# Low parts of split weights made by an accumulating DMA instead of VectorE's subtraction

## Chip, core and metric

The kernel runs on one core of one Trainium2 chip. The metric is the time of one execution on the device, in microseconds (us). A core has TensorE (PE in the profile, with its weight loads as PEld), VectorE (DVE), ScalarE (ACT), GpSimd (POOL) and SyncE (SP), which here issues the loads.

## What is computed

One layer of a diffusion backbone: a half-step SwiGLU feed-forward block, a token mixer (latent attention beside a gated chunk MLP), and a second half-step SwiGLU block. The change touches only weights of the two feed-forward blocks:

```python
def swiglu(h, w1, w3, w2):
    return (jax.nn.silu(h @ w1) * (h @ w3)) @ w2

def ffn_sublayer(h_in, shift, scale, gate, norm_w, w1, w3, w2):
    h = modulate(rms_norm(h_in, norm_w), shift, scale)
    return h_in + 0.5 * gate * swiglu(h, w1, w3, w2)
```

The model width is 1024 and the hidden width 2816, that is 22 blocks of 128. The first block works on 768 tokens (512 latent, 256 context), the second on the 512 latent ones. Everything is float32.

## The kernel before

**Split operands.** TensorE is fed in the type fp32r, which keeps fewer bits than float32. To keep the precision, every operand is held as a pair: a high part (the value rounded to fp32r) and a low part (the value minus its high part). A product is three matmuls (`mm3`): high by high, high weight by low activation, low weight by high activation. The third is the first that needs the weight's low part.

**Pairs.** `Stream.operand` makes the pair of one weight piece of 128x512: ScalarE copies the piece into the high tile (`oph`), and VectorE subtracts the high tile from the piece into the low tile (`opl`). There are five buffers of each (`OPS`), used in rotation. The piece comes from a `raw` buffer (three of them, 128x1024, so two pieces each) that SP fills from `wst` in memory, or from a `block` buffer (two of them, 128x2048) in the stages below.

**Order.** `Flow` is a queue of pieces to be made. At each slot of TensorE's work, `fill` makes as many new pairs as the slot before used up, so up to five pairs are alive, and the slot takes its pairs from the front. In the feed-forward stages every engine's instructions keep the order in which the program is written.

**Stages that the change touches.**
- *Plain up projections.* Hidden blocks 2 and 3 of the first feed-forward block (`plain_wants`): two weights of two pieces each, so 2 x 2 x 2 = 8 pairs. Each pair serves 24 matmuls. Before them come two hidden blocks that run while the inputs arrive; their results are taken over by ScalarE and VectorE (`evac_first`) at the start of this stage.
- *Down projections.* After some of the hidden blocks, a group of them is multiplied with its part of `w2` (`down_wants`, `down_flow`). The first feed-forward block has groups of 5, 5 and 6 hidden blocks in this form, the second 4, 4, 4, 4 and 2. A group of n takes 2n pairs, so 32 and 36 pairs.

**Stages around them.** The other hidden blocks use a Strassen-Winograd form (`Winograd`): from a `block` of four pieces GpSimd makes sums and differences (four additions for each hidden block: `s`, then three in place in `block`), all seven results are split with `Stream.operand`, and seven products are run. The wants of the down groups stand in the same `Flow` queue, behind the last two pieces of a hidden block. GpSimd issues no transfer in the kernel before.

Of the kernel before, what the change touches and what calls it, by code (L numbers as in the profile page):

```python
# [12 lines left out]
AF = mybir.ActivationFunctionType  # L13
ALU = mybir.AluOpType
# [103 lines left out]
class Stream:  # L118
# [19 lines left out]
    def split(self, dst, src, eng=None):  # L138
        self.pin(self.nc.scalar.copy(dst[0], src))
        self.pin((eng or self.nc.vector).tensor_sub(dst[1], src, dst[0].bitcast(F32)))  # L140
        return dst

    def pair(self):
        return [self.op_pool.tile([P, 512], F32R, tag=f"op{p}", bufs=self.op_bufs, name=f"op{p}_{self.nc.next_id()}") for p in "hl"]
# [29 lines left out]
def layer_kernel(ctx: ExitStack, tc: tile.TileContext, xT, wfirst, wst, wada, wuq, wkpe, cols, wrope, vnw, rope, out):  # L174
# [7 lines left out]
    st = Stream(nc, raws, opp, OPS, wst)  # L182
# [81 lines left out]
    u0, rw0 = st.raw_pool.tile([P, 2048], F32, tag="block", bufs=BLOCKS, name="block_first"), st.raw()  # L264
# [48 lines left out]
    def ada_row(r, d, kts=range(NK)):  # L313
        n = 2 * P if d in ROWS2 else P
        o = pa[0:2, :n]
        for kt in kts:
            pin(nc.tensor.matmul(o, sc[:, kt, :], r[:, kt * n : kt * n + n], start=kt == 0, stop=kt == NK - 1))
        return o
# [210 lines left out]
    for k in range(NK):  # L529
# [13 lines left out]
        if later:  # L543
            o = ada_row(units[k + 2][0], k + 2)
# [82 lines left out]
    def down_wants(flow, n, u0):  # L627
        raw = []

        def want(p):  # L630
            if p % 2 == 0:
                raw[:] = [st.half(wst, u0 + p // 2)]
            return st.operand(raw[0][:, p % 2 * 512 : p % 2 * 512 + 512])

        for p in range(2 * n):
            flow.todo.append(lambda p=p: want(p))
# [27 lines left out]
    U_UP1, U_DN1, U_IN = 0, 44, 66  # L664
# [233 lines left out]
    flow = Flow(OPS)  # L898
# [3 lines left out]
    def plain_wants(f):  # L902
        for w in range(2):
            raw = []

            def first(w=w, raw=raw):
                raw[:] = [st.half(wst, U_UP1 + 2 * f + w)]
                return st.operand(raw[0][:, :512])

            flow.todo.append(first)  # L910
            flow.todo.append(lambda raw=raw: st.operand(raw[0][:, 512:]))

    for f in range(NFIRST, NPLAIN1):
        plain_wants(f)
# [166 lines left out]
    def in_want(i, w):  # L1081
        if w == 0:
            inw[i].append(st.half(wst, U_IN + i))
        src = inw[i][0][:, w * 512 : w * 512 + 512]
        inw[i].append(homes[2] if i == 2 and w else st.pair())
        hi, lo = inw[i][-1]
        nc.scalar.copy(hi, src)
        return lambda: nc.vector.tensor_sub(lo, src, hi.bitcast(F32))

    TILES = (0, 1, 2, 1, 2, 1, 1, 0)  # L1090
    for dt in range(NK):
        w = in_want(dt - 5, 0) if dt > 4 else None
# [212 lines left out]
    def v_norm(t, pt):  # L1305
        gv = ut[:, t, :]
        nc.scalar.activation(gv, pt, AF.Gelu_apprx_tanh)
        sq = p1.tile([P, 512], F32, tag="t3", name=f"sqg{t}")
        nc.scalar.activation(sq, gv, AF.Square)
        g4 = gv.rearrange("p (a b) -> p a b", a=4)  # L1310
        nc.gpsimd.tensor_mul(g4, g4, vw)
        m8 = p1.tile([P, 8], F32, tag="m8", name=f"m8g{t}")
        nc.vector.tensor_reduce(m8, sq.rearrange("p (h d) -> p h d", d=64), axis=AX.X, op=ALU.add)
        nc.vector.tensor_scalar(m8, m8, 1.0 / 64, EPS, ALU.mult, ALU.add)
        nc.gpsimd.tensor_tensor(m8, m8, nhalf, ALU.pow)
        vn = gv.rearrange("p (h d) -> p h d", d=64)
        nc.vector.tensor_mul(vn, vn, bc(m8.unsqueeze(2), [P, 8, 64]))
        split((vnh[:, t, :], vnl[:, t, :]), gv)
# [72 lines left out]
    def gate_t(j):  # L1391
        pt = mm()
        for t in range(4):
            nc.tensor.transpose(pt[:, t * P : t * P + P], ut[:, t, j * P : j * P + P], ident)
        split((mixh[:, j, :], mixl[:, j, :]), pt)
# [253 lines left out]
    def diffs(i):  # L1649
        hA1, hA2, hB1, hB2 = hfA[:, i, :], hfA[:, i + 4, :], hfB[:, i, :], hfB[:, i + 4, :]  # L1650
        nc.vector.tensor_sub(hA1, hB1, hA1)
        nc.vector.tensor_sub(hB1, hB2, hB1)
        nc.vector.tensor_sub(hB2, hB2, hA1)
        nc.vector.tensor_sub(hA2, hA2, hB2)
        split([d[:, i, :] for d in T1], hA1)
        split_shift([d[:, i, :] for d in T2], hB2, mod_s[2][0][:, i + 4 : i + 5])
# [37 lines left out]
    flow = Flow(OPS)  # L1694
# [142 lines left out]
```

## Time and profile before

| | |
|---|---|
| median of 3 runs | 1162.75 us (1162.31 to 1163.12) |
| the profiled execution's own time: its span, first to last instruction | 1160.9 us |
| the median stands above the span by | 1.85 us |
| instructions in the span | 18702 |
| transfers by SP and others, mean rate | 125.89 MB, 108 GB/s |

The page gives the busy time of each engine; TensorE's matmuls overlap, and their ends are modelled, so its busy share says little on whether it runs at its full rate. The number of matmuls that start in a window says more. In a timeline row stand the start, the duration, the engine, the line of the program, the operation and the tiles (out<-in), and in brackets the idle time of the engine before it and what ended it. Lines of the program that go through one helper are all shown as L60.

### The profile page before, as it was taken

What the parts mean: (1) busy time and instruction counts of PE and PEld (TensorE: products, weight loads), DVE (VectorE), ACT (ScalarE), POOL (GpSimd) and SP (SyncE); (2) the same over time, 40 slices, a digit from 0 to 9 for tenths busy, and PEclk for the clock granted to TensorE, in tenths of its full rate; (3) what the DMA queues carried; (4) which work ended last, traced back from release to release, by engine and by line L of the source; (5) the groups of instructions that cost most, each with busy time, mean ns of one, the idle gap of its engine ahead of it and who ended that gap; (6) DMA issues with size and microseconds to landing.
All of it is one profiled execution on the core that took longest, in us unless ns stands there. A gap on an engine that the chain in (4) does not pass through costs nothing. (4 is left out here: it accounts for less than half of the span.)

```text
span 1160.9 us, 18702 instructions
## 1 busy us (share of the span) xinstructions
PE 1139.5 (98%) x7070; PEld 1071.9 (92%) x7070; DVE 906.1 (78%) x1668; ACT 532.0 (46%) x1075; POOL 320.9 (28%) x279
## 2 busy tenths in 40 slices
PE   9999999999999999999999999999999999999998
PEld 5699999999999999999988788999999989898997
DVE  4778799889888779866746969869876959686884
ACT  4455431441244213444745549876543535353441
POOL 0011401320333013300017637670013325142330
PEclk9999999999999999999999999999999999999999
DMA  9441244334334664412242111002221322333312
GB/s 351 146 140 37 91 145 137 119 127 164 110 127 145 210 209 158 144 57 82 82 144 90 57 37 55 19 1 76 72 92 55 132 87 74 109 110 109 110 37 91
DMA packets 34650, 125.89 MB, mean 108 GB/s; under 512 B 3584, under 2 KB 10496, under 8 KB 29056
## 3 DMA queue, kind: packets, MB, share of 16 engines
q1 hardware_dynamic: 34416, 124.63, 31.3%
q8 instruction: 56, 0.92, 0.3%
q14 instruction: 34, 0.28, 0.1%
q10 hardware_dynamic: 144, 0.06, 0.0%
HBM read 122.58 MB, written 2.10 MB: 107 GB/s over the span
## 5 line engine op out<-in xcount | busy, mean ns | idle before, releaser
L60 DVE TENSOR_TENSOR opl<-block,oph 128x512 fp32r<-128x512 f32 x216 | 190.6, 888 | 35.5 <-ACT oph L60 33.4
L60 POOL TENSOR_TENSOR block<-block 128x512 f32<-128x512 f32 x70 | 103.7, 1481 | 393.5 <-DVE opl L60 390.8
L60 ACT CAST oph<-block 128x512 fp32r<-128x512 f32 x216 | 134.0, 621 | 144.6 <-PE mm L60 91.7
L60 PE MATMUL mm<-gh,oph 128*128 128x384 f32 (+1 forms) x440 | 155.2, 353 | 0.0
L60 PE MATMUL mm<-gl,oph 128*128 128x384 f32 (+1 forms) x440 | 154.9, 352 | 0.0
L60 PE MATMUL mm<-gh,opl 128*128 128x384 f32 (+1 forms) x440 | 154.9, 352 | 0.0
L60 DVE SCALAR_TENSOR_TENSOR x<-mm,g,x 128x256 f32<-128x256 f32 (+2 forms) x184 | 83.0, 490 | 49.9 <-PE mm L60 49.3
L60 ACT CAST oph<-raw 128x512 fp32r<-128x512 f32 x106 | 64.4, 619 | 93.8 <-PE mm L60 68.0
L60 PEld LDWEIGHTS mm<-gh,opl 128*128 128x128 f32 x440 | 82.6, 188 | 5.7
L60 PEld LDWEIGHTS mm<-gh,oph 128*128 128x128 f32 x440 | 82.6, 188 | 5.6
L60 PEld LDWEIGHTS mm<-gl,oph 128*128 128x128 f32 x440 | 82.6, 188 | 5.5
L60 DVE TENSOR_TENSOR opl<-raw,oph 128x512 fp32r<-128x512 f32 x106 | 73.2, 704 | 9.5 <-ACT oph L60 9.0
L60 POOL TENSOR_TENSOR s<-block 128x512 f32<-128x512 f32 x35 | 52.3, 1495 | 101.8 <-DVE gl L60 73.3
L60 POOL TENSOR_TENSOR block<-s,block 128x512 f32<-128x512 f32 x35 | 47.5, 1357 | 77.0 <-DVE opl L60 76.6
L60 PE MATMUL mm<-hl,oph 128*128 128x384 f32 x192 | 64.6, 336 | 1.8 <-DVE hl L60 1.8
L60 PE MATMUL mm<-hh,oph 128*128 128x384 f32 x192 | 64.5, 336 | 0.0
L60 PE MATMUL mm<-hh,opl 128*128 128x384 f32 x192 | 64.3, 335 | 0.0
L60 DVE SCALAR_TENSOR_TENSOR junk<-raw,cb 128x1024 bf16<-128x1024 f32 x48 | 60.3, 1263 | 0.1
L60 PE MATMUL one<-hh,oph 128*128 128x384 f32 x144 | 48.7, 338 | 0.0
L60 PE MATMUL one<-hl,oph 128*128 128x384 f32 x144 | 48.7, 338 | 0.0
L60 PE MATMUL one<-hh,opl 128*128 128x384 f32 x144 | 48.6, 337 | 0.0
L60 DVE SCALAR_TENSOR_TENSOR raw<-raw,cb 128x1024 f32<-128x1024 f32 x32 | 41.0, 1289 | 7.7 <-DMA raw<-wada 7.4
(649 smaller groups left out, 3461.6 us busy)
## 6 DMA issues: line engine op xcount, KB each, us to landing
raw<-wst SPq DMA_DIRECT2D x77, 512.0 KB, 3.7
block<-wst SPq DMA_DIRECT2D x36, 1024.0 KB, 4.9
raw<-wada SPq DMA_DIRECT2D x56, 512.0 KB, 4.0
block<-wada SPq DMA_DIRECT2D x7, 1024.0 KB, 7.4
x<-xT SPq DMA_DIRECT2D x6, 512.0 KB, 6.7
raw<-wfirst SPq DMA_DIRECT2D x8, 256.0 KB, 6.4
out<-x SPq DMA_DIRECT2D x7, 256.0 KB, 2.2
block_first<-wada SPq DMA_DIRECT2D x2, 512.0 KB, 8.0
```

What stands on the lines that cost most here:

```text
L60: return lambda *a, **k: self.tc.keep_in_program_order(f(*a, **k))
```

## The change

For the pairs of the plain up projections and of the down groups, the low part is no longer a VectorE subtraction. ScalarE writes the negated piece, rounded to fp32r, into the low tile, then copies the piece into the high tile. A transfer issued by GpSimd's queue then reads the same piece of the weight from memory once more and adds it onto the low tile: minus the rounded value plus the value. The 8 + 32 pairs of the first feed-forward block and the 36 of the second go this way, 76 in all. The other pairs (those from `block`, of the last down groups and of the middle stages) are made as before.

```diff
+    def sum_split(self, dst, src, dram):
+        self.pin(self.nc.scalar.activation(dst[1], src, AF.Copy, scale=-1.0))
+        self.pin(self.nc.scalar.copy(dst[0], src))
+        self.pin(self.nc.gpsimd.dma_start(dst[1], dram, accum_op=ALU.add))
+        return dst
+
+    def quarter_of(self, u, w):
+        o = (u % 2) * 1024 + w * 512
+        return self.dram[u // 2][:, o : o + 512]
...
     def down_wants(flow, n, u0):
...
-            return st.operand(raw[0][:, p % 2 * 512 : p % 2 * 512 + 512])
+            return st.sum_split(st.pair(), raw[0][:, p % 2 * 512 : p % 2 * 512 + 512], st.quarter_of(u0 + p // 2, p % 2))
...
     def plain_wants(f):
...
-                return st.operand(raw[0][:, :512])
+                return st.sum_split(st.pair(), raw[0][:, :512], st.quarter_of(U_UP1 + 2 * f + w, 0))
...
-            flow.todo.append(lambda raw=raw: st.operand(raw[0][:, 512:]))
+            flow.todo.append(lambda raw=raw, w=w: st.sum_split(st.pair(), raw[0][:, 512:], st.quarter_of(U_UP1 + 2 * f + w, 1)))
```

## Prediction

> **What bounds the kernel now.** I read the page's busy times first, then windows of 20 us, then what TensorE waited for.
>
> ```profile
> PE 1139.5 (98%) x7070; PEld 1071.9 (92%) x7070; DVE 906.1 (78%) x1668; ACT 532.0 (46%) x1075; POOL 320.9 (28%) x279
> ...
> 160.00:180.00 20.00, 20.00 (x117) 20.00 (x116) 19.20 (x43) 4.35 (x8) 0.00 (x0) 1.00 0.47 155
> 400.00:420.00 20.00, 20.00 (x117) 20.00 (x116) 13.82 (x31) 3.44 (x6) 0.00 (x0) 1.00 0.66 219
> 900.00:920.00 20.00, 18.98 (x159) 18.81 (x158) 17.91 (x32) 10.18 (x23) 10.24 (x8) 1.00 0.31 106
> 1060.00:1080.00 20.00, 20.00 (x108) 17.32 (x107) 11.21 (x16) 5.37 (x10) 5.45 (x4) 1.00 0.12 40
> ...
> PE one L60 <- ACT oph L60: 2.1, 2, 1.1
> PE mm L60 <- DVE hl L60: 1.8, 2, 0.9
> PE big L60 <- DVE sl L60: 1.6, 1, 1.6
> ```
>
> In each window stand the busy time of PE, PEld, DVE, ACT and POOL with their instructions, the granted clock, and the transfers' share. In the first feed-forward block (160 and 400 us) 117 matmuls start in 20 us whether VectorE is 19.2 or 13.8 us busy. TensorE sets the pace there, and less work on VectorE buys nothing. The down groups of the second block (1060) leave VectorE idle for 9 of 20 us; its products (900) bring both near their limits. The waits at the end are all that I can find of the touched blocks' stalls: 5.5 us. So VectorE's share of 78% is not a bound that the change lifts, and the question is whether the low parts still come in time.
>
> **What goes and what comes, on each engine.**
>
> ```profile
> L60 DVE TENSOR_TENSOR opl<-raw,oph 128x512 fp32r<-128x512 f32 x106 | 73.2, 704 | 9.5 <-ACT oph L60 9.0
> L60 ACT CAST oph<-raw 128x512 fp32r<-128x512 f32 x106 | 64.4, 619 | 93.8 <-PE mm L60 68.0 <-DMA raw<-wst 10.9 <-PE one L60 5.2
> 71.76 0.60 ACT L60 ACTIVATE sl<-big 128x512 f32<-128x512 f32 x1 [1.82 <-PE big L524]
> SPq L135 <- DVE opl L60: 180.6, 42, 19.1
> ```
>
> VectorE loses 76 subtractions of 0.704 us, 53.5 us, nearly all beside a TensorE at its own pace: worth nothing by itself. ScalarE gains 76 activations of 128x512; the one in the trace takes 0.60 us, so 46 us, on an engine at 46% that waits for TensorE in the row of its own casts. These too lie beside other work, but each puts the high copy behind it 0.6 us later. The negated copy takes the high copy's old place, so the time from which the transfer may start is the old end of the high copy. The `raw` buffer is now given back by ScalarE, not by VectorE, about 0.7 us earlier; SP's loads, which waited for VectorE 42 times, start that much sooner, and nothing on the path waits for them.
>
> **The transfer's length** is the unknown on which everything hangs: from the end of the negated copy to the moment when TensorE may load the low part. No accumulating transfer and none from GpSimd is in the trace. The nearest rows, with size and median time from issue to landing:
>
> ```profile
> raw<-wst SPq DMA_DIRECT2D x77, 512.0 KB, 3.7
> block<-wst SPq DMA_DIRECT2D x36, 1024.0 KB, 4.9
> out<-x SPq DMA_DIRECT2D x7, 256.0 KB, 2.2
> x<-vnw SPq DMA_DIRECT2D x1, 256.0 KB, 3.7
> ```
>
> The shortest is 2.2 us, a plain store of the same 256 KB. A plain load of 256 KB takes 3.7. From 512 to 1024 KB the landing grows by 1.2, so a second reading of 256 KB (the transfer must also read what it adds onto) is 0.6. GpSimd has to issue it: SP's issue rows are 0.33 us, GpSimd's own instructions 1.3 to 1.7, and I take 1.0. That gives 3.7 + 0.6 + 1.0 = 5.3 us. The upper end is 7.0: a plain load and a store after it one behind the other (3.7 + 2.2), with the issue, 6.9. I take 5.3 because reading from memory is what the two 3.7 rows have in common with it.
>
> DMA: Bandwidth & Descriptors (the Trainium skill), section "Anatomy of one DMA", gives 2.0 us plus bytes over 436 GB/s for a GpSimd transfer, and its section "Specifications" puts the first byte at about 1 us; by these 256 KB would be an estimated 3.6 us, and the sum below about 0.9 instead of 2.8. The trace's 3.7 for a load that SP issues without any addition speaks for more; no row here shows a transfer of GpSimd.
>
> **Where it is waited for: the first two plain pairs.**
>
> ```profile
> 73.64 2.90 ACT L60 CAST oph<-raw 128x512 fp32r<-128x512 f32 x5
> 74.38 5.30 DVE L60 TENSOR_TENSOR opl<-raw,oph 128x512 fp32r<-128x512 f32 x5
> 76.15 0.34 PE L60 MATMUL mm<-hh,opl 128*128 128x384 f32 x1
> 78.23 0.33 PE L60 MATMUL mm<-hh,opl 128*128 128x384 f32 x1
> 84.47 0.33 PE L60 MATMUL big<-hh,opl 128*128 128x384 f32 x1
> ```
>
> Here five pairs are made at once and the first is taken at once. The first copy ends at 73.64 + 0.62 = 74.26, and TensorE wants the low part at 76.15: a lead of 1.9 us. With 5.3 TensorE stands still for 3.4 us. The second negated copy ends at about 73.64 + 3 x 0.58 = 75.4; it lands at 80.7, or at 81.2 if it queues for its issue, and is wanted at 78.23 + 3.4 = 81.6: covered. The third is wanted at 84.47: covered by far.
>
> Part of this comes back 12 us later:
>
> ```profile
> 88.11 0.34 PE L60 MATMUL big<-hh,opl 128*128 128x384 f32 x1
> 90.02 0.44 PE L60 MATMUL big<-hh,oph 128*128 128x384 f32 x1 [1.57 <-DVE sl L60]
> 89.41 0.55 DVE L60 TENSOR_TENSOR sl<-big,sl 128x384 f32<-128x384 f32 x1
> ```
>
> TensorE stops until VectorE has read the bank just finished. Its last matmul ends at 88.45, VectorE comes only at 89.41, because it is behind. With TensorE 3.4 us later and two subtractions fewer in between, VectorE comes at once; ScalarE's added copies (1.2 us) are covered by the same 3.4. Of the 0.96 us I take back 0.8.
>
> **The down groups.** In each group the first pair has the shortest lead (end of its copy to the first low matmul):
>
> ```profile
> 152.34 0.62 ACT L60 CAST oph<-raw 128x512 fp32r<-128x512 f32 x1 [0.95 <-ACT oph L60]
> 160.93 0.33 PE L60 MATMUL mm<-gh,opl 128*128 128x384 f32 x1
> 857.17 0.62 ACT L60 CAST oph<-raw 128x512 fp32r<-128x512 f32 x1 [0.42 <-PE mm L60]
> 863.32 0.39 PE L60 MATMUL mm<-gh,opl 128*128 128x512 f32 x1
> 920.58 0.62 ACT L60 CAST oph<-raw 128x512 fp32r<-128x512 f32 x1
> 927.10 0.39 PE L60 MATMUL mm<-gh,opl 128*128 128x512 f32 x1
> 1090.68 1.35 ACT L60 CAST oph<-raw 128x512 fp32r<-128x512 f32 x2
> 1096.36 0.39 PE L60 MATMUL mm<-gh,opl 128*128 128x512 f32 x1
> ```
>
> The first block's group has 160.93 - 152.96 = 8.0 us; its two others repeat the same sequence. Of the second block's five, the first has 5.5, the second 5.9, and the last (the first of two copies in its row ends 0.62 after 1090.68) 5.06; the two between repeat the second's order of work, and I count them like it. At 5.3 only the last is short, by 0.24. Later pairs are made one slot after another, four ahead, and have more.
>
> **GpSimd's queue.** In the down groups the transfers stand between additions that are two pieces of work away, and each issue waits for a ScalarE copy that is due anyway. The one addition that is really moved is that of the first `block`: in the program it stands behind all eight plain transfers, and in the trace it ran ahead of its place.
>
> ```profile
> 74.55 1.67 POOL L60 TENSOR_TENSOR s<-block 128x512 f32<-128x512 f32 x1 [73.26 <-DVE gl L60]
> 76.30 1.62 POOL L60 TENSOR_TENSOR block<-block 128x512 f32<-128x512 f32 x1
> 93.33 0.61 ACT L60 CAST oph<-raw 128x512 fp32r<-128x512 f32 x1
> 96.46 1.48 POOL L60 TENSOR_TENSOR block<-s,block 128x512 f32<-128x512 f32 x1 [18.54 <-DVE opl L60]
> 102.58 1.13 ACT L60 CAST oph<-block 128x512 fp32r<-128x512 f32 x2
> ```
>
> The last of the eight copies ends at 93.94. Behind it come 1.0 for the issue and 1.67 + 1.62 + 1.48 for three additions, so 99.7, and ScalarE reads the result at 102.58: hidden, with 2.9 us to spare. If that cover goes, it is VectorE, busy through this stretch, that is late next.
>
> **Sum.** 3.4 - 0.8 + 0.24 = +2.8 us. The profiled span goes from 1160.9 to 1163.7; the median stands 1.85 above it, so 1165.6 us, +0.25%. A difference of 0.2% (2.3 us) is about what a measurement of this kernel can tell from no change.
>
> **Rivals.**
>
> *A: the transfer is short, and the result is not slower.* Place: the matmul at 76.15. The stall costs less than 2.3 us if the length is below 1.9 + 0.8 + 2.3 = 5.0. At 3.7, the plain row, it is 3.7 - 1.9 - 0.8 = +1.0: 1163.75. For it: the two load rows are no longer than that. Against it: they have neither the addition nor GpSimd's issue. The rule of the skill's page on DMA falls into this case.
>
> *B: VectorE's relief shows, and it is faster.* With a transfer like the store (2.2 us) the first stall is 0.3 against 0.8 given back; should the lighter VectorE also remove the other waits above (1.8 and 2.1 us), the gain is 0.5 + 3.9 = 4.4: 1158.4. Against it: the wait of 1.8 is for `hl`, far behind the last plain pair, and that of 2.1 is for ScalarE's copies in products, where no subtraction goes.
>
> *C: the transfer is long.* From 5.5 us on, the second block's groups stall one after the other. At 7.0: 5.1 - 0.8 at the start, and 1.5 + 3 x 1.1 + 1.9 = 6.7 in the groups, together +11.0: 1174. For it: the first transfer meets a queue that has not run before and loads in flight. Against it: nothing in the page shows 256 KB taking so long outside the crowded start.
>
> **How the numbers follow.** The forecast, a length of 5.0 to 6.5, has 0.42, and gives 1165.1 to about 1171; C beyond that 0.15; A 0.32; B 0.11. So slower 0.57, same 0.32, faster 0.11. The range runs from a length of 2.2 without B's further gain (2.2 - 1.9 - 0.8 = -0.5: 1162.3) to C's 1174; what is left out is most of B and the end of C.
>
> **What would show it.** VectorE near 853 us, ScalarE near 578, `opl<-raw` down from 106 in that group. TensorE waiting about 3.4 us in one piece near 76 us, and less than 1.2 near 91. In the issue rows a line `opl<-wst` of 256 KB with 3.7 to 5.5 us to landing. First low matmuls of the second block's groups without a wait, but for the last. No wait at 76 would refute the length; waits in every group of the second block would put it above 6; waits elsewhere would mean that GpSimd's order or the loads are late, which I count as hidden.

## The result and the profile after

The changed kernel takes 1208.28 us (median of 4 runs, 1202.45 to 1211.45), against 1162.93 us for the kernel before (median of 4 runs, 1162.31 to 1163.21). The ratio is 1.038, with an interval of 1.036 to 1.041: 45 us slower, where 1165.6 and at most 1174 was forecast. The profiled execution took 1207.46 us with a span of 1205.6 us, 44.7 us above that of before.

The page's busy times, and from the groups those of the instructions that the change touches (busy time, mean ns of one, idle time ahead and what ended it):

```profile
PE 1154.7 (96%) x7070; PEld 1077.9 (89%) x7070; DVE 858.9 (71%) x1592; ACT 570.1 (47%) x1151; POOL 389.2 (32%) x355
```

```profile
L60 POOL DMA_DIRECT2D opl<-wst x76 | 66.3, 872 | 245.4 <-ACT opl L60 167.4 <-PE mm L527 74.9 <-issue 1.7
L60 ACT ACTIVATE opl<-raw 128x512 fp32r<-128x512 f32 x76 | 48.0, 632 | 97.2 <-PE mm L60 65.4 <-DMA raw<-wst 31.6
L60 DVE TENSOR_TENSOR opl<-raw,oph 128x512 fp32r<-128x512 f32 x30 | 19.9, 686 | 4.0 <-ACT oph L60 3.7
```

The work moved as meant: VectorE 47 us lighter, ScalarE 38 us heavier, 76 issues on GpSimd of 0.87 us each. The transfers are another matter. In the view of the transfers a queue's row gives packets, MB and the share of 16 engines' span; an issue row gives the size and the median time from issue to landing:

```profile
q1 hardware_dynamic: 34416, 124.63, 30.8%
q0 software_dynamic: 10944, 19.93, 9.7%
...
raw<-wst SPq DMA_DIRECT2D x77, 512.0 KB, 4.3
raw<-wada SPq DMA_DIRECT2D x56, 512.0 KB, 5.7
opl<-wst POOLq DMA_DIRECT2D x76, 256.0 KB, 8.4
```

The new transfers (queue q0) land after 8.4 us in the median. They hold the engines 9.7% of the span for 19.93 MB, 5.9 us of all 16 engines for a MB (0.097 x 1205.6 / 19.93); SP's loads (q1) hold them 3.0 us for a MB. And SP's loads are later too: `raw<-wada`, the loads of the conditioning weights, stood at 4.0 before.

What TensorE and VectorE waited for, after (us in total, times, longest; VectorE's wait for `raw<-wada` was 7.4 us in 6 times before):

```profile
PE mm L60 <- DMA opl<-wst: 24.1, 13, 3.8
PE mm L60 <- DVE x L60: 5.3, 2, 3.7
...
PE big L60 <- DVE sl L60: 0.7, 1, 0.7
...
DVE raw L60 <- DMA raw<-wada: 26.0, 7, 6.4
```

TensorE waits 24.1 us for low parts, in 13 places. The head of the second block's first down group, that is its first pair, shows one of them, in the timeline (start, duration, engine) and in windows (busy PE, PEld, DVE, ACT, POOL with their instructions, granted clock, transfers' share; packets overlap, so a share may exceed 1):

```profile
878.18 0.63 ACT L60 ACTIVATE opl<-raw 128x512 fp32r<-128x512 f32 x1 [0.55 <-PE mm L60]
878.38 0.33 SPq L127 DMA_DIRECT2D block<-wst  x1
879.16 0.95 POOL L60 DMA_DIRECT2D opl<-wst  x1 [1.43 <-ACT opl L60]
880.78 3.21 SPq L135 DMA_DIRECT2D raw<-wst  x2
887.52 0.79 PE L60 MATMUL mm<-gh,opl 128*128 128x512 f32 x1 [3.15 <-DMA opl<-wst]
892.63 0.39 PE L60 MATMUL mm<-gh,opl 128*128 128x512 f32 x1
```

```profile
880.00:884.00 4.00, 4.00 (x35) 3.93 (x33) 1.39 (x5) 3.62 (x9) 2.35 (x4) 1.00 0.87 256
884.00:887.50 3.50, 0.37 (x2) 0.00 (x0) 1.56 (x4) 1.72 (x4) 1.21 (x2) 1.00 1.02 256
887.50:891.00 3.50, 3.48 (x8) 2.80 (x9) 0.00 (x0) 0.00 (x0) 0.00 (x0) 0.51 1.10 274
```

The transfer is issued 0.8 us after SP has started a load of 1 MB, and two more of 512 KB follow at once; such loads that start close together are called a burst below. It lands 8.3 us later, and TensorE stands for 3.15 us. Then comes the second price: for the next 3.4 us the granted clock is 0.51, and the same matmul takes 0.79 us and not 0.39. Such half-clock stretches sum to 27.3 us in the changed kernel and to 3.4 in the one before. At half speed that is (27.3 - 3.4) / 2 = 12 us lost, if TensorE would have been busy throughout. One of the seven stretches of the changed kernel, at 58 us, lies ahead of its first transfer.

SP's burst is no product of the change. It stands in the trace of before, at the same place:

```profile
851.00:855.00 4.00, 4.00 (x36) 4.00 (x35) 2.77 (x6) 3.25 (x7) 0.00 (x0) 1.00 0.02 4
855.00:859.00 4.00, 4.00 (x35) 4.00 (x35) 2.68 (x6) 1.91 (x4) 1.63 (x1) 1.00 0.14 20
859.00:863.00 4.00, 4.00 (x35) 4.00 (x34) 3.00 (x7) 2.07 (x6) 0.00 (x0) 1.00 0.94 360
863.00:867.00 4.00, 4.00 (x20) 3.27 (x19) 3.47 (x8) 1.95 (x5) 0.00 (x0) 1.00 0.40 145
```

**Where the 44.6 us arise.** All these kernels have the same 7070 matmuls in the same order, so the n-th matmul of one can be set against the n-th of before. The table gives what each stretch adds to the lag (how much later a matmul starts than in the kernel before), in us, with the time of before at which the stretch ends. E1 to E10 are the experiments of the next section. FFN1 and FFN2 are the first and the second feed-forward block, "first" to "fifth" their down groups; "FFN1 third" is the third group with what follows it.

```
stretch (end, us of before)   after   E1    E2    E3    E4    E5    E6    E7    E8    E9   E10
start (71.6)                   +1.6  +0.1  -0.2  -0.3  -0.3  -0.2   0.0  +0.1   0.0  -0.2  +0.1
plain pairs (114.0)            +4.9  +5.5  -0.8  +2.0  +1.3  +2.8   0.0  -0.8   0.0  -0.3   0.0
to FFN1 first (159.5)          -0.2  +1.1  +2.2   0.0  +0.7  +2.5   0.0  +1.3  -1.6   0.0  -1.6
FFN1 first (211.5)             +1.8  +2.4   0.0  +0.6   0.0  +8.2   0.0   0.0   0.0   0.0   0.0
FFN1 second (305.1)            +2.3  +2.0   0.0  +1.5  +0.5  +7.1   0.0   0.0   0.0   0.0   0.0
FFN1 third (471.5)            +10.1  +9.6 +12.8  +0.6  +2.2 +12.9  +9.8   0.0   0.0   0.0   0.0
between the blocks (846.8)     +0.3  +0.1  +0.4  +1.8  +0.1  +0.1  +0.5  +0.3  +1.5  +0.3   0.0
FFN2 first (885.8)             +5.0   0.0  +0.1  +2.0  +0.7  +1.7   0.0  +0.4   0.0   0.0   0.0
FFN2 second (955.4)            +3.9  -0.7  -0.5  +3.7  +3.9  +5.1  -0.7  +0.1  -1.5  -0.6  -1.4
FFN2 third (1017.8)            +4.7  -0.6  -0.1  +0.5  +1.3  +1.4  -0.8  -0.7  -1.6  -1.2  -1.5
FFN2 fourth (1079.5)           +3.7  +0.1  +0.3  +5.3  +1.9  +5.1  -0.2  +0.7  -0.8  -0.4  -0.7
FFN2 fifth (1120.9)            +6.3  +0.1  +0.9  +4.7  +2.2  +5.4  -0.2  +0.1  -0.3  -0.3  -0.3
rest (1157.5)                  +0.2   0.0  +0.4  +0.2  +0.3  +0.1  +0.1  +0.1  -0.1   0.0  -0.1
sum to the last matmul        +44.6 +19.6 +15.4 +22.6 +14.8 +52.2  +8.5  +1.6  -4.2  -2.7  -5.5
```

Three kinds of place carry it: the plain pairs (4.9), the heads of the down groups (4.1 in the first block's first two groups, 23.6 in the second block's five), and the first block's third group (10.1). Entries of about 1.6 in the start, before FFN1 first and between the blocks come and go with half-clock stretches that also fall where no transfer is near; nothing is read from them.

### The profile page after: what moved, and what is told of

The parts are those of the page before. It is cut to its first block, busy times and chain, and to the rows that moved or that the text cites. A ratio compares the mean times of both kernels' runs of the same rounds, so it can differ in the third digit from the quotient of the medians.

```text
span 1205.6 us, 18855 instructions
## 1 busy us (share of the span) xinstructions
PE 1154.7 (96%) x7070; PEld 1077.9 (89%) x7070; DVE 858.9 (71%) x1592; ACT 570.1 (47%) x1151; POOL 389.2 (32%) x355
## 3 DMA queue, kind: packets, MB, share of 16 engines
q0 software_dynamic: 10944, 19.93, 9.7%
## 5 line engine op out<-in xcount | busy, mean ns | idle before, releaser
L60 DVE TENSOR_TENSOR opl<-block,oph 128x512 fp32r<-128x512 f32 x216 | 187.7, 876 | 33.2 <-ACT oph L60 31.1
L60 PE MATMUL mm<-gh,opl 128*128 128x384 f32 (+1 forms) x440 | 159.9, 363 | 20.4 <-DMA opl<-wst 20.3
L60 PE MATMUL mm<-gh,oph 128*128 128x384 f32 (+1 forms) x440 | 159.1, 362 | 5.3 <-DVE x L60 5.3
L60 PE MATMUL mm<-gl,oph 128*128 128x384 f32 (+1 forms) x440 | 158.4, 360 | 0.0
L60 POOL DMA_DIRECT2D opl<-wst x76 | 66.3, 872 | 245.4 <-ACT opl L60 167.4
L60 ACT ACTIVATE opl<-raw 128x512 fp32r<-128x512 f32 x76 | 48.0, 632 | 97.2 <-PE mm L60 65.4
```

The source lines that it names most:

```text
L60: return lambda *a, **k: self.tc.keep_in_program_order(f(*a, **k))
```

## The experiments

The theory after the result: the transfer's length is set by what SP has on the DMA engines at the same moment, and in the first block's third group the transfers in turn delay SP's loads. The rival: the transfers are long by themselves (GpSimd's queue, the addition, the second read from memory, each other). E1 to E4 had one run each beside one of the kernel before at 1161.41; E5 to E8 stand beside a median of 1161.81 for it, E9 and E10 beside 1161.98. E7 and E9 were timed in 10 runs, the others in one.

### E1: only the first block's 40 pairs

```diff
 def want(p):
+    if not (u0 < U_UP2):
+        return st.operand(src)
     return st.sum_split(...)
```

> Only the 40 pairs of the first feed-forward block go through the transfer; the 36 of the second block's down groups are made by VectorE as before. Theory (each burst of transfers pays once, at its head, because it meets SP's block and raw loads, and TensorE's clock is halved for 3.4 us after each long stop): the second block's five waits and their halved stretches are gone, 16.5 + 8.5 = 25 us of the 45, so about 1182 us; no low-part wait after 800 us; the wait for x near 446 us and its halved clock stay. Rival (transfers slow the kernel as a whole, through memory or queues): the loss shrinks by less than half of that, over 1195 us, with waits spread.

1182.25 us. The second block's lag goes from +23.6 to -1.1, and what is left, about 20 us, lies in the first block as in the changed kernel. The stretches add up: nothing global, such as a heavier ScalarE, is at work.

### E2: not the first two pairs of a group

The first two pairs of every down group, and the first two plain ones, are made by VectorE; 58 of 76 go by transfer.

```diff
+    if not (p >= 2):
+        return st.operand(src)
```

> In every down group the first two pairs, and the first two plain pairs, are made by VectorE; all others go through the transfer (58 of 76). Theory: what costs is the short lead of the head of a burst; third pairs had leads of 7.7 to 10 us before, against transfers of 8 to 9 us among SP's loads, so waits of 0 to 1.5 us in the second block's groups and none in the first's, about 1165 to 1174 us, the upper part if the wait for x near 446 us (5.3 us and a halved stretch) stays. Rival (the transfers' total volume): the loss goes with the number of transfers, 58/76 of 45 us, so about 1197 us.

1178.13 us, above what the theory gave (1165 to 1174). The heads are gone: plain pairs -0.8, the second block +0.7 in all, though its transfers still take 5.8 to 8.9 us. But the third group of the first block has +12.8. That loss isn't at the head, and the theory had not separated it.

### E3: only the first pair of each group

9 of 76: the first pair of each down group and the first plain one.

```diff
+    if not (p == 0):
+        return st.operand(src)
```

> Only the first pair of each down group and the first plain pair go through the transfer (9 of 76); all others by VectorE. It separates what lengthens the first transfer. Theory (SP's block and raw loads, which start at the same moment): the first transfer still takes 7 to 8 us from issue to landing in the second block, TensorE waits 2 to 3.5 us per group there, about 1163 + 17 + 9 = 1185 to 1192 us. Rival (its own followers in GpSimd's queue share the engines with it): alone it lands in 4 to 5.5 us, no waits in the down groups, 3 us at the plain stage, about 1166 us.

1185.33 us. With no second transfer anywhere near, the heads still stop TensorE:

```profile
PE mm L60 <- DMA opl<-wst: 17.3, 9, 3.8
...
opl<-wst POOLq DMA_DIRECT2D x9, 256.0 KB, 7.9
```

The eight at the heads land 6.6 to 9.0 us after their issue; the plain one, with no burst of SP beside it, after 4.2. So at the heads the followers aren't the cause (the rival's 1166). The third group of the first block costs only 0.6: there it is the number of transfers that counts.

### E4: the transfer overwrites instead of adding

This leaves the addition out: the low tile then holds the weight itself, not its low part.

```diff
-        self.pin(self.nc.gpsimd.dma_start(dst[1], dram, accum_op=ALU.add))
+        self.pin(self.nc.gpsimd.dma_start(dst[1], dram))
```

> The transfer writes the weight piece, rounded, over the low tile and does not add (the low parts are then not what they should be; the time is read). All 76, with the same waits and the same issue by GpSimd. Theory (the addition doubles what a transfer does on the engines, but the collision with SP's loads is the larger part): landing 6 to 7 us in the bursts, half of the waits left, about 1180 us. Rival 1 (the addition is all): transfers of 4 us, about 1165 us. Rival 2 (GpSimd's issue is what takes long): landing unchanged at 8 us, over 1200 us.

1177.59 us: about a third of the loss is left.

```profile
q0 software_dynamic: 10944, 19.93, 6.0%
...
opl<-wst POOLq DMA_DIRECT2D x76, 256.0 KB, 5.7
```

Without the addition the same bytes take 6.0% and not 9.7% of the engines, 3.5 us for a MB, and the landing falls from 8.4 to 5.7. The issue is shorter too, 0.54 us. So the addition makes each byte about 1.7 times as dear. But a plain write meets the same burst: the second block still loses 10.

### E5: what is added comes from the buffer on the chip

```diff
-        self.pin(self.nc.gpsimd.dma_start(dst[1], dram, accum_op=ALU.add))
+        self.pin(self.nc.gpsimd.dma_start(dst[1], src, accum_op=ALU.add))
```

> All 76 pairs by transfers, but what is added is read from the raw buffer on the chip and not from memory a second time (the buffer is then held until the transfer has landed). Theory (length is the addition at the target, at twice the engine time for a byte, and the sharing with SP's loads): the transfers keep 7 to 9 us in the median and the total stays within 1195 to 1215, with some loads later because of the held buffers. Rival (the second read from memory makes it long): the first plain transfer lands under 3.7 us after the negated copy, the waits at the heads of the groups shrink by half or more, total below 1185.

1214.86 us.

```profile
q0 software_dynamic: 10944, 19.93, 9.6%
...
opl<-raw POOLq DMA_DIRECT2D x76, 256.0 KB, 6.3
```

```profile
PE mm L60 <- DMA opl<-raw: 18.2, 9, 3.8
PE mm L60 <- DVE gl L60: 12.1, 3, 4.9
...
SPq L135 <- DMA opl<-raw: 195.2, 37, 11.7
```

A transfer alone is shorter (3.4 us in the plain stage from 84 us on), so reading the piece from memory and not from the chip is worth 0.7 to 0.8 us (4.1 in E8 and 4.2 in E3, also alone). The engine time is the same 9.6%, and the heads still take 6.5 to 8.9. The kernel is no faster: `raw` is now held until the transfer has landed, and SP's next loads wait for that 37 times. The first block's groups lose 7 to 13 us each, with a new wait of 12.1 us for `gl`; that the later loads bring this wait about is likely, but no run separates it. The median of 6.3 was below the 7 to 9 that I had put down; the time and the heads were as the theory had them.

### E6: only the first block's third group

```diff
+    if not (u0 >= U_DN1 + 10 and u0 < U_UP2):
+        return st.operand(src)
```

> Only the 12 pairs of the first block's third down group go by transfers. Theory (there the engines are already two thirds busy with the loads of the conditioning weights; the transfers fill them, those loads land 3 us later each, VectorE, which takes its work in order, comes late with the group's results, and TensorE waits for it): 8 to 13 us lost, nearly all after the group's first third, behind waits of VectorE for these loads; total 1169 to 1175. Rival (the lateness is built up by the two groups before, which take part of the same loads): under 4 us lost, total below 1166.

1171.34 us: 12 pairs alone cost 9.8 us in that stretch, so the two groups before have no part in it. The way is seen in the changed kernel: its timeline, its transfers between 395 and 435 us, and its window at 400 us.

```profile
447.34 1.22 DVE L60 SCALAR_TENSOR_TENSOR raw<-raw,cb 128x1024 f32<-128x1024 f32 x1 [6.43 <-DMA raw<-wada]
449.77 1.39 DVE L60 SCALAR_TENSOR_TENSOR x<-mm,g,x 128x256 f32<-128x256 f32 x4
450.66 0.66 PE L60 MATMUL mm<-gh,oph 128*128 128x384 f32 x1 [3.74 <-DVE x L60]
```

```profile
raw<-wada SPq DMA_DIRECT2D x10, 512.0 KB, 7.3
opl<-wst POOLq DMA_DIRECT2D x9, 256.0 KB, 8.3
```

```profile
400.00:420.00 20.00, 19.17 (x109) 18.53 (x108) 10.75 (x23) 5.22 (x10) 3.45 (x4) 1.00 0.96 261
```

In this group two pieces of the conditioning weights are due at each slot, and the engines were 0.66 busy in that window before. The transfers bring that to 0.96; the loads land after 7.3 us, not 4.6. VectorE, which takes its work in the order of the program, waits 6.43 us for one. Only then does it add the finished bank into `x`, and TensorE needs that bank back. E4 fits: its transfers hold the engines for less time, and this stretch loses 2.2 us and not 10.1.

### E7: neither the heads nor the third group

48 of 76 pairs by transfer.

```diff
+    if not (p >= 2 and not U_DN1 + 10 <= u0 < U_UP2):
+        return st.operand(src)
```

> 48 of the 76 pairs go by transfers: none of the first two of a group, none of the first two plain ones, none of the first block's third group. If the loss is made up of the heads of the groups and of the third group's conditioning loads alone, 2 to 3 us are left: 1163 to 1165, a ratio of 1.001 to 1.003. Rival (the transfers also load ScalarE, GpSimd or the engines everywhere): the third group was only where it showed, and the total stays above 1170.

1164.30 us against 1161.81 (10 and 13 runs): ratio 1.0021, interval 1.0006 to 1.0035. TensorE has no wait for a transfer left, and 48 transfers of 7.5 us median cost next to nothing. The theory holds to the size: without the places that it names, 43 of the 45 us are gone.

### E8 and E10: SP's loads out of the way

E8 sends only the second block's five first pairs by transfer, and cuts SP's loads in that block to an eighth of their columns, once each buffer has been filled. E10 is its control: the same cut loads and no transfer at all. In both the second block computes with old weights.

```diff
+        t, w = tiles[seen % n], src.shape[-1] // 8
+        self.nc.sync.dma_start(t[:, :w], src[:, :w])
+        return t
```

> Only the first pair of each of the second block's five down groups goes by a transfer (5 of 76), and in the second block SP's loads are cut to an eighth of their columns once each of its buffers has been filled (the results are then of old weights; the instructions of the other engines are the same). With full loads these five pairs, together with the first block's, cost the second block about 16.5 us. Theory (the transfer shares the DMA engines with the 1 MB and two 512 KB loads that SP starts at the head of each group): groups two to five lose their waits, the transfer lands about 5 us after the negated copy, total 1161 to 1166, any rest in the first group, where three loads are still full. Rival (GpSimd's queue or the addition itself is slow there): the transfers still take 7 to 9 us and the total is 1175 to 1180.

> The control for the run with cut loads: SP's loads in the second block cut to an eighth in the same way (old weights), and no pair made by a transfer, so all 76 by VectorE's subtraction. If the five transfers at the heads of the groups cost nothing once SP's loads are out of the way, this gives the same as with them, 1157 to 1160.5; if they still cost some 1 us each, it is 5 us less, 1152 to 1155.

1158.53 and 1157.18 us. E8 lies below the range that was put down for it (1161 to 1166), because the cut loads make the kernel faster by themselves, as E10 shows. In E8:

```profile
opl<-wst POOLq DMA_DIRECT2D x5, 256.0 KB, 4.1
raw<-wst SPq DMA_DIRECT2D x19, 64.0 KB, 1.9
```

The same five transfers at the same heads now land after 4.1 us, and the negated copy's end to landing is 4.4 to 4.6. TensorE comes 0.8 to 1.0 us later and never waits. In the second block's groups E8 gains 4.1 us on the kernel before and E10 3.9: the transfers cost nothing there. The 1.4 us between the two totals lie in front of the second block, where E8 has a half-clock stretch at 658 us and no transfer is near. This settles what makes the heads late: SP's loads, not GpSimd's queue, the addition or the read by themselves. The addition makes it worse, since without it (E4) the same loads cost the second block 10 us and not 23.6.

### E9: what the change could bring at the most

The transfer is left out altogether; ScalarE's negated copies stay in the low tiles, which therefore aren't the true low parts.

```diff
-        self.pin(self.nc.gpsimd.dma_start(dst[1], dram, accum_op=ALU.add))
```

> All 76 pairs as in the change, but the transfer itself is left out: ScalarE's negated copy stays in the low tile (so the low parts are not the true ones), and VectorE's subtractions are gone. This is what the change could bring at the most, with a transfer that costs nothing. Theory (TensorE sets the pace, VectorE's 53 us and ScalarE's 46 us lie beside it): a gain of the wait of 1 us at 88 to 90 us and at most the other waits of VectorE and ScalarE, 1157.5 to 1162, ratio 0.996 to 1.000. Rival (VectorE's relief is worth a good part of its 53 us): below 1150. Other rival (the added copies on ScalarE are themselves on the path): above 1164.

1160.35 us against 1161.98 (10 and 13 runs): ratio 0.9984, interval 0.9971 to 0.9998. With VectorE at

```profile
PE 1138.7 (98%) x7070; PEld 1071.5 (93%) x7070; DVE 858.8 (74%) x1592; ACT 570.7 (49%) x1151; POOL 321.6 (28%) x279
```

47 us less of VectorE's work, with 39 us more of ScalarE's, are worth 1.6 us. That bounds what a transfer in this place can bring, however short; of the versions run here that do the whole work none is faster than the kernel before.

## Why the prediction was wrong, point by point

- **TensorE sets the pace, and VectorE's relief is worth nothing: right.** E9 measures it at 1.6 us. VectorE came to 858.9 us (853 forecast), ScalarE to 570.1 (578).
- **GpSimd's issue, 1.0 us: right** (0.87). The addition that it pushed back stayed hidden: it ended at 106.2 us, and ScalarE read the result at 110.85. The -0.2 us up to the first down group is a balance, though. The kernel before has a half-clock stretch at 123 us that the changed one hasn't (worth 1.6 by E8 and E10), and TensorE loses 1.3 us at 117 to 121 us of before, mainly behind VectorE's `hl` (2.3 us of waits, 1.8 before). The prediction had named VectorE as late next; no run separates why it is.
- **The first plain pair: right in place, and in size by luck.** TensorE waited 3.46 us, 3.4 forecast; the transfer took 5.45 us from the end of the negated copy, 5.3 forecast. But 5.3 was a sum for a transfer alone, and with no other transfer behind it (E3) this one took 4.5 and TensorE waited 2.51. The rest of the 5.45 goes with what runs beside it in the changed kernel, the pairs that follow and a load that SP issues at 77.4 us, and the sum had neither. The second to the fifth pair's transfers landed 8.2 to 10.1 us after their issue. So the second pair waited 0.39 where I had it covered. The 0.8 us given back at the `sl` wait came (1.6 to 0.7); E7, where TensorE doesn't stop before it, has the same 0.7, so the stop was not needed for it.
- **The length taken as one number: this is the step that failed.** 5.3 us was put together from a median over the whole kernel and one single load, and applied at every head. Alone it's even too long: 4.4 to 4.6 in E8. Of its parts, the addition was 0.9 where I had 0.6 (4.1 from issue in E8, 3.2 without it in E4 at 942 us, where SP has nothing in flight), and 0.35 of that is the longer issue. At the heads of the second block it was 8.7, 8.4, 8.9, 7.8 and 8.7 us. The rest of the step held: those lengths less the leads of the prediction give 3.2, 2.5, 3.0, 1.9 and 3.6, and TensorE waited 3.15, 2.83, 3.23, 2.25 and 3.78. I had read the transfers' share in windows of 20 us (0.31 and 0.12 in that block), which average a burst away; in windows of 4 us the same trace of before shows 0.94 where the first transfer would fall. Rival C named the mechanism, one group stalling after the other, with loads in flight as a ground, and stopped at 7.0 us and 1174. Its other ground, a queue that has not run before, is worth 0.2 us at most (4.3 from issue for the first of E8's five transfers, 4.1 for the last).
- **The price of a stop: a term that was missing.** I counted a wait at its own length. In the changed kernel 24.1 us of waits for low parts and 5.3 for `x` came with 12 us at half clock. Stops of 2.75 and 2.9 us, measured from one matmul's start to the next, were followed by a stretch of 3.4 us at half clock (E6 at 428, E4 at 934 us); stops of 2.65 and 2.85 us were not (after at 1088, E3 at 76), and nor was one of 3.0 us (E6 at 456). TensorE: Matmul & The Clock Gate (the Trainium skill), section "HAM oscillation — how this bites in real kernels", sets the bound at gaps of over about 3.4 us; these rows put it lower, and not at one sharp value.

The windows behind the stops of E4 (2.9), E3 (2.85) and E6 (2.75 and 3.0), with the granted clock third from the end:

```profile
937.10:940.50 3.40, 3.20 (x8) 2.52 (x9) 0.00 (x0) 0.00 (x0) 0.00 (x0) 0.50 1.00 331
78.50:81.90 3.40, 3.37 (x19) 3.37 (x20) 2.71 (x5) 0.90 (x2) 0.00 (x0) 1.00 0.67 234
430.50:433.90 3.40, 2.93 (x9) 2.96 (x10) 0.97 (x4) 0.00 (x0) 0.00 (x0) 0.50 0.92 195
459.50:462.90 3.40, 3.40 (x20) 3.40 (x21) 2.63 (x5) 0.62 (x1) 1.61 (x1) 1.00 0.82 310
```

- **The loads that run beside it: a cover that I named and didn't price.** "Hidden" was right of SP's loads of weights. It was wrong of the conditioning weights in the first block's third group, 9.8 us by E6. The row of the window at 400 us, with 0.66, stood in the prediction; 12 transfers are 3.15 MB and at 5.9 us for a MB 18.6 us of all engines, a third of the 55 us from their first issue to their last landing (393 to 447 us), on top of 0.66. I used that row for TensorE's pace alone.
- **The rule for a GpSimd transfer.** DMA: Bandwidth & Descriptors (the Trainium skill), section "Anatomy of one DMA", gives an estimated 2.6 us for 256 KB, and the prediction added the first byte of its section "Specifications" to an estimated 3.6. A plain write alone lies between them (3.2 us from issue, E4 at 942 us); an adding one alone takes 4.1 (E8), and beside a burst 6.6 to 9.0 (E3). The measurement decides: the rule is near for a transfer alone, and not for one beside a burst.

## What to carry to other kernels

A transfer's length is a property of the moment: before a transfer is put on a path with a few us of lead, lay its start against the other queues' bursts, in windows no longer than the transfer itself. Count engine time, not bytes: a transfer that adds is dearer than its size, and where the engines are two thirds busy it takes its time from loads that somebody else waits for, in order. And price a stop of TensorE of about 3 us at its own length and often 1.7 us more for the half clock behind it (2.7 behind the longest stop here, where the stretch was 6.8 us and began within the stop).

## What was not expected of the hardware

An adding transfer of GpSimd's queue holds the engines 5.9 us for a MB, a plain one of the same queue 3.5, and SP's loads, in packets twice as large, 3.0. Where it adds from makes no difference to that (9.7% from memory, 9.6% from the chip), only 0.7 to 0.8 us to the landing of a transfer alone. Issuing an adding transfer costs GpSimd 0.87 us, a plain one 0.54.
